# A hybrid retention, delta-rule and latent-attention trunk: SiLU kept until the next tile's copy, squares by chunk, three banks for projections, modulation jobs moved out of the attention

## The chip, the cores and the metric

The kernel runs on one core of a Trainium2 chip. The metric is the device time of one execution in microseconds, the median of several runs. TensorE does the matrix products, VectorE and ScalarE the elementwise work, GpSimd some additions; SyncE's queue issues most transfers. Below they are PE, DVE, ACT, POOL and SP in rows of the profile.

## What is computed

The reference is a trunk of two layers over 512 latent tokens and 256 context tokens of width 2048. In each layer a modulated norm is followed by one input projection, three groups of heads, a gate, one output projection and a residual with a modulated gate:

```python
shift, scale, gate = jnp.split(jax.nn.silu(c) @ ada_w[i] + ada_b[i], 3, axis=-1)
shift_c, scale_c, gate_c = jnp.split(jax.nn.silu(c_ctx) @ ada_w[i] + ada_b[i], 3, axis=-1)
h = rmsnorm(x, norm_w[i]) * (1.0 + scale[:, None]) + shift[:, None]
hc = rmsnorm(xc, norm_w[i]) * (1.0 + scale_c) + shift_c
zl = split_cols(h @ w_in[i], IN_SPLITS)
zc = split_cols(hc @ w_in[i], IN_SPLITS)
ret_c, ret_l = retention_mixer(...)
gdn_c, gdn_l = gated_deltanet_mixer(...)
mla_c, mla_l = mla_mixer(...)
x = x + gate[:, None] * (jnp.concatenate([ret_l, gdn_l, mla_l], axis=-1) @ w_out[i])
if not last:
    xc = xc + gate_c * (jnp.concatenate([ret_c, gdn_c, mla_c], axis=-1) @ w_out[i])
```

The delta group runs a centred convolution of five taps and a SiLU over its queries, keys and values, a chunked delta rule in both directions with their outputs added, a norm over the head and a SiLU gate. In the last layer the context is not projected for queries and gates, since only the latent tokens are an output.

## The kernel before, in words

Everything lies transposed: a tile has 128 channels on the partitions and the 768 tokens along the row, first the 256 of the context, then the 512 latent ones. A projection of 128 columns takes 16 tiles of the 2048 inputs. Each fp32 operand is split in a high and a low part (`split`, line 234 on ScalarE and 235 on VectorE), and three products are accumulated: a `zl` matmul of 512 columns (line 291) and, where the context is wanted, a `zc` matmul of 256 (line 293) for each.

Each layer has three stages: the mixing stage (`phase_a`), the latent attention (`phase_b`) and the output projection with the next layer's norm (`phase_c`). In the mixing stage every projection is a task, a generator that yields after each of its 16 steps (`proj_steps`): convolutions of the delta heads (`conv_task`), gates (`gate`), latent queries and keys (`latent`), retention inputs (`ret_raw`, `ret_v`). The heads' own code (`gdn_head`, then `ret_head`) calls `pump(us)` between its steps, which pulls about so many microseconds of projection steps from the tasks in their order, and `need(...)`, which runs the named tasks to their end. So TensorE has projection matmuls between the dependent steps of a head. The instructions then go through a scheduler that works by the program's order and its own model of durations; each engine carries out its list in order.

A head of the delta group ends in a chain of six steps (`chain`), in each of which two chunks of 128 tokens are finished, one per direction; the second to come to a chunk adds into `on` (line 1001, VectorE). `out_norm` then squares `on` by chunk (line 684, ScalarE), takes the root (396 to 401), scales (695, VectorE), and after `pump(6)` turns it (`ot`, line 692, TensorE).

A finished projection is copied out of its bank: the latent part by ScalarE (line 393, for convolutions 778), the context part by VectorE. A gate then runs its SiLU (413 to 421: four ScalarE and two VectorE instructions) and is stored; a convolution is first multiplied and added (780 on ScalarE, 782 four times on VectorE). Projections of the mixing stage take PSUM banks from a ring of four, `pza`; `m` tiles have four more banks.

The modulation of the next layer is computed on the side, in 64 jobs (`ada_job`): 16 multiplies on ScalarE (line 496), seven or eight additions on GpSimd (line 498) and four loads of 256 KB each. After each four jobs their sums are closed and turned by small matmuls. Jobs are called from projections in the mixing stage of layer 0 (36 calls), in its attention (16) and in its output projection (14). The first 16 jobs are the residual gate of layer 0, 32 the shift and scale of layer 1, the last 16 the residual gate of layer 1.

## Time and profile before

| quantity | value |
|---|---|
| runs of the kernel | median 3235.6 us of 3 (3230.44 to 3240.53) |
| the profiled execution | 3233.15 us, span 3231.4 us |
| TensorE's mean granted clock | 0.976 of full speed |
| TensorE busy | 3057.6 us, 95% of the span |
| VectorE, ScalarE, GpSimd busy | 2034.7 us (63%), 1639.7 us (51%), 701.9 us (22%) |
| stages: start, mixing 0, attention 0, output 0 | to 191, to 1320, to 1623, to 1906 us |
| stages: mixing 1, attention 1, output 1 | to 2713, to 3022, to the end |

The span runs from the first to the last instruction of the profiled execution. An engine is busy while an instruction of its own runs; matrix products are pipelined, so a busy TensorE may still run at a lower clock. A wait is an idle time of an engine, named after the instruction that came after it and what released that. In a table by stretch each line gives the stretch, its length, the busy time of PE, PEld (weight loads), DVE, ACT and POOL with the number of their instructions, then TensorE's granted clock as a share of full speed, the busy share of the DMA engines and their GB/s. In a table of groups a line gives line, engine, operation, output and inputs, shapes and count, then busy time and mean ns of one, then idle time of the engine just before them.

### The profile page before, as it was taken

How to read it: one execution, taken by the hardware profiler on the slowest of the kernel's cores; microseconds unless marked ns; L12 is line 12 of the kernel's file. 1: busy time of each engine (PE TensorE's matmuls, PEld its weight loads, DVE VectorE, ACT ScalarE, POOL GpSimd, SP SyncE). 2: the span in 40 equal slices, each digit the busy share in tenths (PEclk: the TensorE clock that was granted, in tenths of full speed). 3: DMA queues.
4: the chain of work that ended last, by engine and by line, in shares of the span. 5: the costliest groups of instructions: out<-in, count | busy, mean ns of one | idle time of the engine just before them, and what ended most of it. 6: DMA issues, size and time to landing. Idle time of an engine off the chain costs nothing.

```text
span 3231.4 us, 50867 instructions
## 1 busy us (share of the span) xinstructions
PE 3057.6 (95%) x18925; PEld 2582.6 (80%) x18925; DVE 2034.7 (63%) x3512; ACT 1639.7 (51%) x3492; POOL 701.9 (22%) x487
## 2 busy tenths in 40 slices
PE   7988979899899999999999999999999999999998
PEld 3477868788778778888878887888898887888887
DVE  3268567585675676676763265766766667766634
ACT  4266264453645666677776355352515245544533
POOL 0026043241344442255577300000000000000000
PEclk8999989999899999999999999999999999999999
DMA  8765243342344555333475443332424256512434
GB/s 286 254 207 144 52 145 92 87 133 71 121 123 134 162 179 179 109 107 106 140 228 160 121 120 95 91 98 69 119 58 124 66 157 177 155 52 64 134 113 132
DMA packets 506447, 417.06 MB, mean 129 GB/s; under 512 B 46454, under 2 KB 436694, under 8 KB 506198
## 3 DMA queue, kind: packets, MB, share of 16 engines
q1 hardware_dynamic: 505875, 413.70, 42.9%
q8 instruction: 148, 2.42, 0.3%
q14 instruction: 101, 0.83, 0.1%
q0 software_dynamic: 96, 0.02, 0.0%
q10 hardware_dynamic: 227, 0.08, 0.0%
HBM read 349.82 MB, written 63.88 MB: 128 GB/s over the span
## 4 chain that ended last, share of the span: by engine, by line
PE 48%; ACT 2%; DVE 1%; DMA 1%; issue 1%; POOL 1%; SPq 0%; ACTq 0%; DVEq 0%; POOLq 0%
PE zl L291 16%; PE zlc L291 9%; PE vz L274 4%; PE zc L293 3%; PE sc L1288 2%; PE zlc L293 2%; PE oacc L1347 2%; PE zt L282 2%; DMA gb<-g_d 1%; PE ptp L1340 1%; PE f L291 1%; POOL ada_a L498 1%; PE racc L1105 1%; PE chain L974 0%; PE f L293 0%
## 5 line engine op out<-in xcount | busy, mean ns | idle before, releaser
L498 POOL TENSOR_TENSOR ada_a<-ada_a,ada_p 128x512 f32<-128x512 f32 x480 | 699.9, 1458 | 1114.5 <-ACT ada_p L496 789.3
L235 DVE TENSOR_TENSOR wl<-raw,wh 128x512 fp32r<-128x512 f32 x632 | 477.6, 761 | 265.7 <-ACT wh L234 230.1
L291 PE MATMUL zl<-hh,wh 128*128 128x512 f32 (+1 forms) x1440 | 591.8, 411 | 8.8 <-ACT cz L778 7.0
L291 PE MATMUL zl<-hl,wh 128*128 128x512 f32 (+1 forms) x1440 | 578.0, 401 | 1.0 <-DVE hl L235 1.0
L291 PE MATMUL zl<-hh,wl 128*128 128x512 f32 (+1 forms) x1440 | 577.9, 401 | 0.0
L234 ACT CAST wh<-raw 128x512 fp32r<-128x512 f32 x632 | 373.2, 605 | 274.3 <-PE zc L293 134.2
L496 ACT ACTIVATE ada_p<-araw,const_f 128x256 f32<-128x256 f32 x960 | 423.8, 503 | 61.2 <-DMA araw<-in_ada_w_dram 46.5
L291 PEld LDWEIGHTS zl<-hh,wh 128*128 128x128 f32 (+1 forms) x1440 | 274.1, 190 | 66.7 <-ACT cz L778 7.4
L291 PEld LDWEIGHTS zl<-hl,wh 128*128 128x128 f32 (+1 forms) x1440 | 273.4, 190 | 60.5 <-DVE hl L235 2.5
L291 PEld LDWEIGHTS zl<-hh,wl 128*128 128x128 f32 (+1 forms) x1440 | 273.2, 190 | 60.5 <-issue 0.8
L293 PE MATMUL zc<-hh,wh 128*128 128x256 f32 (+1 forms) x960 | 280.1, 292 | 0.0
L293 PE MATMUL zc<-hh,wl 128*128 128x256 f32 (+1 forms) x960 | 277.3, 289 | 0.0
L293 PE MATMUL zc<-hl,wh 128*128 128x256 f32 (+1 forms) x960 | 277.2, 289 | 0.0
L293 PEld LDWEIGHTS zc<-hh,wh 128*128 128x128 f32 (+1 forms) x960 | 183.8, 191 | 3.9 <-issue 2.5
L293 PEld LDWEIGHTS zc<-hh,wl 128*128 128x128 f32 (+1 forms) x960 | 182.9, 191 | 3.0 <-issue 2.5
L293 PEld LDWEIGHTS zc<-hl,wh 128*128 128x128 f32 (+1 forms) x960 | 183.2, 191 | 1.7 <-issue 0.8
L291 PE MATMUL zlc<-ml,wh 128*128 128x512 f32 x448 | 178.0, 397 | 2.7 <-DVE ml L235 2.7
L291 PE MATMUL zlc<-mh,wl 128*128 128x512 f32 x448 | 178.0, 397 | 0.0
L291 PE MATMUL zlc<-mh,wh 128*128 128x512 f32 x448 | 177.8, 397 | 0.0
L782 DVE SCALAR_TENSOR_TENSOR cy<-cz,const_f,cy 128x770 f32<-128x770 f32 (+1 forms) x96 | 113.2, 1180 | 25.0 <-ACT cy L780 23.8
L291 PEld LDWEIGHTS zlc<-ml,wh 128*128 128x128 f32 x448 | 84.3, 188 | 24.5 <-DVE ml L235 5.4
L291 PEld LDWEIGHTS zlc<-mh,wh 128*128 128x128 f32 x448 | 84.5, 189 | 20.3 <-issue 0.8
(1249 smaller groups left out, 6456.5 us busy)
## 6 DMA issues: line engine op xcount, KB each, us to landing
raw<-in_w_in_dram SPq DMA_DIRECT2D x368, 256.0 KB, 3.7
araw<-in_ada_w_dram SPq DMA_DIRECT2D x256, 256.0 KB, 4.0
raw<-in_w_out_dram SPq DMA_DIRECT2D x144, 256.0 KB, 3.8
ar<-in_ada_w_dram SPq DMA_DIRECT2D x128, 256.0 KB, 5.2
x_d<-xt SPq DMA_DIRECT2D x32, 384.0 KB, 3.2
raw<-in_w_in_dram SPq DMA_DIRECT2D x72, 128.0 KB, 3.0
ret_d<-rw SPq DMA_DIRECT2D x20, 384.0 KB, 3.0
rz<-ret_d SPq DMA_DIRECT2D x20, 384.0 KB, 3.4
```

Of the source, the lines that this page charges most:

```text
L234: S.copy(hi, src)
L235: V.tensor_tensor(out=lo, in0=src, in1=hi.bitcast(F32), op=ALU.subtract)
L274: T.matmul(z[:, 256 * i:256 * i + 256], lhsT=x_[:, (j + i) * P:(j + i + 1) * P], rhs=w, start=first and k == 0 and i == 0, stop=end and k ...
L282: T.matmul(z, lhsT=w, rhs=xx[:, a:b], start=own and first and k == 0, stop=own and last and k == nk - 1)
L291: T.matmul(zl[:m], lhsT=w, rhs=xx[:, NX:], start=st, stop=sp)
L293: i = T.matmul(zc[:m, :NX], lhsT=w, rhs=xx[:, :NX], start=st and zc_open, stop=sp and zc_open)
L496: S.activation(out=pr[:, v], in_=raw[:, i, :], func=AF.Copy, scale=cs32[:, 2 * k + v:2 * k + v + 1])
L498: G.tensor_tensor(out=acc, in0=acc, in1=pr, op=ALU.add)
L782: V.scalar_tensor_tensor(out=y[:, lo:hi], in0=z[:, lo + o:hi + o], scalar=w(2 + o), in1=y[:, lo:hi], op0=ALU.mult, op1=ALU.add)
L1105: T.matmul(acc[:, :NL], lhsT=a[:, sl], rhs=b[:, :NL], start=st and i == 0, stop=sp and i == NCH - 1)
L1288: T.matmul(m[:, po:po + n], lhsT=a[:, qs], rhs=b[:, ko:ko + n], start=i == 0, stop=i == len(ops) - 1)
L1347: T.matmul(acc[:, os], lhsT=a[:, sl], rhs=b[:, js], start=j == 0 and n == 0, stop=j == nk - 1 and n == 2)
```

## The change

- The SiLU of a convolution or a gate, with its store, is kept in a list (`tails`) and issued behind the copy of the next tile that leaves its bank (`flush`), at the end of `need`, or at the end of the stage.
- The convolution's input has a buffer of its own with three parts of 260 columns, so the copy of the latent part becomes two of 258 columns; its result goes to one store instead of two; the zeros at the edges are written behind the previous tile's additions.
- The squares of `on` follow each addition into it. `out_norm` pumps 5 ahead of the scaling and 4 behind it, instead of 6 behind; in the retention heads a `pump(3)` becomes `pump(4)`.
- The mixing stage's projections take their banks from the ring `z` of three. The first groups of a layer use another split of banks.
- The attention calls no jobs. The 16 last jobs then fall into the mixing stage of layer 1.
- `load_params(1)` moves from the start to the head of the mixing stage of layer 0, and row paddings go.

```diff
     def pza(name="z"):
-        return ps.tile([P, 512], F32, name=name, tag="za", bufs=4)
+        return ps.tile([P, 512], F32, name=name, tag="z", bufs=3)
 
...
         hs = []
-        za, zb, zc2 = pm("f1"), ps.tile([P, 512], F32, name="f2", tag="f2", bufs=1), pz("zc2")
-        zs = [(pz("zl"), zc2[:, :NX]), (pz("zl"), zc2[:, NX:] if l < DEPTH - 1 else None),
-              (za[:, :512], zb[:, :NX]), (za[:, 512:], zb[:, NX:512])]
-        spare.append(ps.tile([P, 512], F32, name="spare", tag="spare", bufs=1))
+        f = lambda n: ps.tile([P, 512], F32, name=n, tag="f2", bufs=3)
+        z0, z1, zc2, za, zb, zc3 = pz("zl"), pz("zl"), pz("zc2"), f("f0"), f("f1"), f("f2")
+        zs = [(z0, zc2[:, :NX]), (z1, zc2[:, NX:] if l < DEPTH - 1 else None), (za, zc3[:, :NX]), (zb, zc3[:, NX:512])]
+        if l == 0:
+            spare.append(ps.tile([P, 512], F32, name="spare", tag="spare", bufs=1))
         owner = (1, 2) if l < DEPTH - 1 else (0, 2)
...
             V.tensor_scalar(out=dst[:m, 0:NX], in0=zc[:m, :NX], scalar1=scale, scalar2=None, op0=ALU.mult)
-        S.activation(out=dst[:m, NX:NT], in_=zl[:m], func=AF.Copy, scale=scale)
+        return S.activation(out=dst[:m, NX:NT], in_=zl[:m], func=AF.Copy, scale=scale).ins
 
...
         V.tensor_scalar(out=ngx, in0=ngx, scalar1=-1.0, scalar2=None, op0=ALU.mult)
-        load_params(1)
         return hs
...
 
+            tails, behind = [], [None]
+
+            def flush(ins=None):
+                fs, tails[:] = tails[:], []
+                for f in fs:
+                    if ins is None:
+                        f()
+                    else:
+                        with tc.issue_after(ins):
+                            f()
+
             def gate(c0, j):
                 lo_ctx = not last
                 zl, zc = yield from proj_in(l, c0, hs, lo_ctx)
                 z, e = ev("gz"), ev("ge")
                 lo = 0 if lo_ctx else NX
-                evac(z, zl, zc)
-                silu_mul(z[:, lo:], z[:, lo:], e[:, lo:])
-                dma(out=gate_d[l][j][:, lo:], in_=z[:, lo:])
+                flush(evac(z, zl, zc))
+
+                def tail():
+                    silu_mul(z[:, lo:], z[:, lo:], e[:, lo:])
+                    dma(out=gate_d[l][j][:, lo:], in_=z[:, lo:])
+                tails.append(tail)
 
...
                 lo = 0 if need_ctx else NX
-                evac(e, zl, zc)
+                flush(evac(e, zl, zc))
                 if kind not in accs:
...
 
-            def token_rstd(src, c0, sq, fill_v):
-                ss, y, t = tiny("nss"), tiny("nry"), tiny("nrt")
-                for n in range(c0, NCH):
-                    S.activation(out=sq[:, n * P:(n + 1) * P], in_=src[:, n * P:(n + 1) * P], func=AF.Square,
-                                 accum_out=ss[:, n:n + 1])
+            def square_chunk(src, n, sq, ss):
+                S.activation(out=sq[:, n * P:(n + 1) * P], in_=src[:, n * P:(n + 1) * P], func=AF.Square,
+                             accum_out=ss[:, n:n + 1])
+
+            def token_rstd(src, c0, sq, fill_v, ss=None):
+                y, t = tiny("nry"), tiny("nrt")
+                if ss is None:
+                    ss = tiny("nss")
+                    for n in range(c0, NCH):
+                        square_chunk(src, n, sq, ss)
                 fill_v(ss[:, c0:])
...
 
-            def out_norm(o, lo, wcol, j, fill_v=mean_eps, pump=lambda us: None):
+            def out_norm(o, lo, wcol, j, fill_v, pump, sq, ss=None):
                 c0 = lo // P
                 g = mk("og")
                 dma(out=g[:, lo:NT], in_=gate_d[l][j][:, lo:])
-                sq = mk("osq")
-                r = token_rstd(o, c0, sq, fill_v)
+                r = token_rstd(o, c0, sq, fill_v, ss)
+                pump(5)
                 scale_tokens(sq, o, r, c0)
-                pump(6)
+                pump(4)
                 m = pm("ot")
...
                 zl, zc = yield from proj_in(l, C_GDN + 512 * which + h * P, hs, need, False)
-                z, y, e = (w_(tag, name, n=NPAD) for tag, name in (("ev", "cz"), ("t", "cy"), ("t", "ce")))
-                lo, hi = (2 if need else LPAD), LPAD + NL
-                for o in (0, NX + 2, hi)[0 if need else 1:]:
-                    V.memset(z[:, o:o + 2], 0.0)
+                z, y = wk.tile([P, 1024], F32, name="cz", tag="cv", bufs=2), ev("cy")
+                z3, y3 = (t[:, :3 * n].rearrange("p (k c) -> p k c", k=3) for t, n in ((z, 260), (y, NX)))
+                s0 = 0 if need else 1
+                lo = s0 * NX
                 if need:
-                    V.tensor_copy(z[:, 2:2 + NX], zc[:, :NX])
-                S.copy(z[:, LPAD:hi], zl)
+                    behind[0] = V.tensor_copy(z3[:, 0, 2:258], zc[:, :NX]).ins
+                with tc.issue_after(behind[0]):
+                    for a, b in ((0, 2), (258, 262), (778, 780))[s0:]:
+                        V.memset(z[:, a:b], 0.0)
+                S.copy(z3[:, 1, 2:260], zl[:, :258])
+                flush(S.copy(z3[:, 2, :258], zl[:, 254:]).ins)
                 w = lambda j: parB[:, 12 * j + 4 * which + h:12 * j + 4 * which + h + 1]
-                S.activation(out=y[:, lo:hi], in_=z[:, lo:hi], func=AF.Copy, scale=w(2))
+                S.activation(out=y3[:, s0:], in_=z3[:, s0:, 2:258], func=AF.Copy, scale=w(2))
                 for o in (-2, 2, -1, 1):
-                    V.scalar_tensor_tensor(out=y[:, lo:hi], in0=z[:, lo + o:hi + o], scalar=w(2 + o),
-                                           in1=y[:, lo:hi], op0=ALU.mult, op1=ALU.add)
-                silu_mul(z[:, lo:hi], y[:, lo:hi], e[:, lo:hi])
-                if need:
-                    dma(out=conv_d[l][h][which][:, :NX], in_=z[:, 2:2 + NX])
-                dma(out=conv_d[l][h][which][:, NX:], in_=z[:, LPAD:hi])
+                    i = V.scalar_tensor_tensor(out=y3[:, s0:], in0=z3[:, s0:, 2 + o:258 + o], scalar=w(2 + o),
+                                               in1=y3[:, s0:], op0=ALU.mult, op1=ALU.add)
+                behind[0] = i.ins
+
+                def tail():
+                    silu_mul(y[:, lo:], y[:, lo:], z[:, lo:NT])
+                    dma(out=conv_d[l][h][which][:, lo:], in_=y[:, lo:])
+                tails.append(tail)
 
...
                 St, seen = [None] * 2, set()
+                osq, oss = mk("osq"), tiny("oss")
                 orders = ([0, 1, 2, 3, 4, 5], [1, 0, 5, 4, 3, 2])
...
                                 V.tensor_tensor(out=on[:, sl], in0=on[:, sl], in1=pp[d][:, 3 * P:], op=ALU.add)
+                                square_chunk(on, n, osq, oss)
                         if not end:
                             St[d] = S2[d]
                     pump(1)
                 ahead = gdn_load(h + 1) if h < 3 and need("conv", h + 1) else None
                 out_norm(on, qlo, parB[:, 71:72], 4 + h, lambda ss: V.scalar_tensor_tensor(
-                    out=ss, in0=ss, scalar=1.0 / HD, in1=qv[:, c0:], op0=ALU.mult, op1=ALU.add), pump)
+                    out=ss, in0=ss, scalar=1.0 / HD, in1=qv[:, c0:], op0=ALU.mult, op1=ALU.add), pump, osq, oss)
                 return ahead
...
                     split(ph[:, :w], pl[:, :w], p_[:, :w])
-                    pump(3)
+                    pump(4)
                     for a, b, st, sp in ((vh, ph, True, False), (vh, pl, False, False), (vl, ph, False, True)):
...
                 turn(m, o, qlo // P)
-                out_norm(m, qlo, parB[:, 70:71], h, pump=pump)
+                out_norm(m, qlo, parB[:, 70:71], h, mean_eps, pump, mk("osq"))
 
...
                 owed[0] = max(owed[0], -4.0)
+                flush()
                 return True
...
             mg = lambda a, b: [task(("mg", j), gate(C_MG + j * P, 8 + j)) for j in range(a, b)]
+            if not last:
+                load_params(1)
             gs = kr_ab()
...
                 advance(next(iter(tasks)))
+            flush()
 
...
                         first_half(h + 1, 0)
-                    if u and not last:
-                        ada_job()
                     for _ in range(PARTS[last][u]):
```

The order of the instructions moves at these places.

ScalarE at the end of delta head 0 in layer 0. `on` is the head's output, `nss` and `oss` hold the sums of squares, `ce` and `cz` are convolution tiles, `ada_p` a product of a job. Before:

```order
L413 ACTIVATE ce<-cy 128x770
L496 ACTIVATE ada_p<-araw,const_f 128x256
L414 ACTIVATE ce<-ce 128x770
L415 ACTIVATE ce<-ce,const_f 128x770
L234 CAST wh<-raw 128x512
L417 ACTIVATE ce<-ce 128x770
L684 ACTIVATE osq,nss<-on 128x128 x5
L234 CAST wh<-raw 128x512
L684 ACTIVATE osq,nss<-on 128x128
```

Now:

```order
L801 ACTIVATE cy<-cz,const_f 128x768
L694 ACTIVATE osq,oss<-on 128x128 x2
L1005 COPY vnew<-chain 128x128
L232 CAST wh<-raw 128x512
L1005 COPY vnew<-chain 128x128
L694 ACTIVATE osq,oss<-on 128x128 x2
L395 ACTIVATE nry<-oss 128x6
L396 ACTIVATE nry<-nry 128x6
```

The squares stood behind the SiLU of the third of three convolution tiles; they now stand two by two in the chain (`vnew` is one of its copies), and the root follows the last two.

ScalarE at a convolution tile of layer 0. Before, with copy, product and SiLU of the same tile:

```order
L778 COPY cz<-zl 128x512
L496 ACTIVATE ada_p<-araw,const_f 128x256
L780 ACTIVATE cy<-cz,const_f 128x770
L496 ACTIVATE ada_p<-araw,const_f 128x256 x5
L234 CAST wh<-raw 128x512
L496 ACTIVATE ada_p<-araw,const_f 128x256 x5
L413 ACTIVATE ce<-cy 128x770
L414 ACTIVATE ce<-ce 128x770
L234 CAST wh<-raw 128x512
L415 ACTIVATE ce<-ce,const_f 128x770
L417 ACTIVATE ce<-ce 128x770
```

Now, where lines 412 to 416 are the SiLU of the tile before, and its result of line 801 is left for the next:

```order
L798 COPY cz<-zl 128x258
L799 COPY cz<-zl 128x258
L412 ACTIVATE cz<-cy 128x768
L801 ACTIVATE cy<-cz,const_f 128x768
L413 ACTIVATE cz<-cz 128x768
L495 ACTIVATE ada_p<-araw,const_f 128x256
L414 ACTIVATE cz<-cz,const_f 128x768
L495 ACTIVATE ada_p<-araw,const_f 128x256 x2
L232 CAST wh<-raw 128x512
L416 ACTIVATE cz<-cz 128x768
L495 ACTIVATE ada_p<-araw,const_f 128x256 x6
```

The SiLU behind a copy now reads a `cy` whose four additions on VectorE belong to the tile before.

TensorE where a projection of the mixing stage of layer 0 follows another. Before, with a bank each for `zl_5739` and `zc_5740`:

```order
L291 MATMUL zl_5478<-hl15_1383,wh_5671 128x512
L293 MATMUL zc_5479<-hl15_1383,wh_5671 128x256
L291 MATMUL zl_5478<-hh15_1382,wl_5672 128x512
L974 MATMUL chain_5628<-r_5630,Xt32_5227 128x128
L293 MATMUL zc_5479<-hh15_1382,wl_5672 128x256
L291 MATMUL zl_5739<-hh0_641,wh_5743 128x512
L293 MATMUL zc_5740<-hh0_641,wh_5743 128x256
L291 MATMUL zl_5739<-hl0_642,wh_5743 128x512
```

Now:

```order
L289 MATMUL zl_6138<-hl15_1384,wh_6350 128x512
L291 MATMUL zc_6139<-hl15_1384,wh_6350 128x256
L289 MATMUL zl_6138<-hh15_1383,wl_6351 128x512
L291 MATMUL zc_6139<-hh15_1383,wl_6351 128x256
L289 MATMUL zl_6389<-hh0_642,wh_6393 128x512
L289 MATMUL zl_6389<-hl0_643,wh_6393 128x512
L289 MATMUL zl_6389<-hh0_642,wl_6394 128x512
L289 MATMUL zl_6389<-hh1_650,wh_6393 128x512
L291 MATMUL zc_6390<-hh0_642,wh_6393 128x256
L291 MATMUL zc_6390<-hl0_643,wh_6393 128x256
L291 MATMUL zc_6390<-hh0_642,wl_6394 128x256
```

The `zc` matmuls of a new tile stood between its `zl` matmuls from the first; four `zl` matmuls now come ahead of the first `zc`, whose bank is the one that the tile before leaves.

## Rows read from the trace of the kernel before

**Rows 1.** Table by stage: busy time of each engine, granted clock, DMA share; seven stages, five shown.

```profile
191.00:1320.00 1129.00, 1033.49 (x6742) 894.03 (x6742) 769.36 (x1157) 606.73 (x1338) 395.71 (x267) 0.96 0.42 126
1320.00:1623.00 303.00, 288.39 (x1873) 254.51 (x1872) 222.12 (x398) 228.25 (x513) 159.97 (x115) 0.98 0.38 119
1623.00:1906.00 283.00, 280.28 (x1598) 240.35 (x1598) 118.07 (x153) 152.42 (x320) 140.30 (x95) 0.99 0.52 159
1906.00:2713.00 807.00, 793.54 (x5132) 673.51 (x5131) 547.73 (x1094) 338.57 (x691) 0.00 (x0) 0.99 0.37 104
2713.00:3022.00 309.00, 307.36 (x1784) 264.85 (x1783) 218.89 (x411) 161.50 (x322) 0.00 (x0) 1.00 0.36 105
```

**Rows 2.** TensorE's waits, mixing stage of layer 0: total, times, longest, in us.

```profile
PE ot L692 <- DVE osq L695: 17.4, 4, 14.0
PE ot L692 <- ACT ge L413: 11.8, 1, 11.8
...
PE ktp L692 <- DVE kn L695: 9.8, 3, 6.2
PE vnp L812 <- ACT nry L397: 7.8, 1, 7.8
PE zl L291 <- ACT cz L778: 7.0, 1, 7.0
PE vtp L892 <- DVE vt L885: 6.2, 6, 2.1
PE vtp L905 <- DVE Xt L876: 6.0, 4, 2.0
```

**Rows 3.** TensorE's timeline, end of delta head 0: start, us, instruction, idle time before.

```profile
445.60 0.39 PE L291 MATMUL zl<-hh,wl 128*128 128x512 f32 x1
...
445.95 0.40 PE L291 MATMUL zl<-hh,wh 128*128 128x512 f32 x1
460.30 1.51 PE L692 MATMUL ot<-const_f,osq 128*128 128x128 f32 x6 [13.95 <-DVE osq L695]
```

**Rows 4.** VectorE's timeline, last `on` addition of head 0 and its scaling.

```profile
399.68 0.29 DVE L1001 TENSOR_TENSOR on<-on,chain 128x128 f32<-128x128 f32 x1 [0.86 <-PE chain L996]
...
459.19 0.96 DVE L695 TENSOR_TENSOR osq<-on,nss 128x768 f32<-128x768 f32 x1
```

**Rows 5.** ScalarE's timeline, first of head 0's six squares.

```profile
450.87 0.31 ACT L684 ACTIVATE osq<-on 128x128 f32<-128x128 f32 x1 [1.03 <-DVE cz L421]
```

**Rows 6.** Busy time and granted clock in the 13.5 us behind the gap.

```profile
462.20:475.70 13.50, 13.50 (x78) 11.50 (x77) 11.54 (x23) 11.84 (x35) 2.23 (x2) 0.88 0.43 135
```

**Rows 7.** ScalarE's timeline, copy of a convolution tile out of its bank.

```profile
634.30 0.57 ACT L778 COPY cz<-zl 128x512 f32<-128x512 f32 x1
```

**Rows 8.** TensorE's waits, mixing stage of layer 1.

```profile
PE ot L692 <- DVE osq L695: 7.9, 3, 4.5
```

**Rows 9.** Busy time in the first 444 us of either mixing stage.

```profile
191.00:635.00 444.00, 397.39 (x2610) 341.04 (x2609) 306.81 (x476) 225.95 (x487) 147.14 (x97) 0.94 0.39 112
1906.00:2350.00 444.00, 433.94 (x2733) 363.65 (x2732) 312.76 (x651) 205.03 (x415) 0.00 (x0) 0.99 0.35 97
```

**Rows 10.** The page's groups by cost: the jobs' additions and multiplies.

```profile
L498 POOL TENSOR_TENSOR ada_a<-ada_a,ada_p 128x512 f32<-128x512 f32 x480 | 699.9, 1458 | 1114.5 <-ACT ada_p L496 789.3
...
L496 ACT ACTIVATE ada_p<-araw,const_f 128x256 f32<-128x256 f32 x960 | 423.8, 503 | 61.2 <-DMA araw<-in_ada_w_dram 46.5
```

**Rows 11.** VectorE's groups, mixing stage of layer 0: busy us, mean ns, idle before.

```profile
L235 DVE TENSOR_TENSOR wl<-raw,wh 128x512 fp32r<-128x512 f32 x189 | 163.2, 865 | 90.1 <-ACT wh L234 75.7 <-issue 10.4 <-DMA araw<-in_ada_w_dram 1.6
```

**Rows 12.** VectorE's groups, mixing stage of layer 1.

```profile
L235 DVE TENSOR_TENSOR wl<-raw,wh 128x512 fp32r<-128x512 f32 (+1 forms) x185 | 125.7, 681 | 33.1 <-ACT wh L234 32.8
L782 DVE SCALAR_TENSOR_TENSOR cy<-cz,const_f,cy 128x770 f32<-128x770 f32 (+1 forms) x48 | 44.6, 929 | 12.6 <-ACT cy L780 12.0
```

**Rows 13.** VectorE's timeline, four additions of one convolution in layer 0.

```profile
437.02 6.94 DVE L782 SCALAR_TENSOR_TENSOR cy<-cz,const_f,cy 128x770 f32<-128x770 f32 x4 [2.39 <-ACT cy L780]
```

**Rows 14.** GpSimd's timeline beside them.

```profile
437.53 3.64 POOL L498 TENSOR_TENSOR ada_a<-ada_a,ada_p 128x512 f32<-128x512 f32 x2 [3.44 <-ACT ada_p L496]
```

More of the change, by code (lines that the diff above doesn't have):

```diff
@@ L47 @@
 COVER = (1.25, 1.0)
-LPAD = NX + 4
-NPAD = NT + 8
 def _rope_tables(dim):
@@ L138, in lslot @@
     def lslot(name, dt=F32R):
-        return lp.tile([P, NPAD], dt, name=name, tag="L")[:, :NT]
+        return lp.tile([P, NT], dt, name=name, tag="L")[:, :NT]
     BUFS = {"t": 5, "ev": 4, "p": 6, "d": 4, "xr": 1, "lacc": 1}
     def w_(tag, name, dt=F32, n=NT):
-        return wk.tile([P, NPAD * 4 // mybir.dt.size(dt)], dt, name=name, tag=tag, bufs=BUFS[tag])[:, :n]
+        return wk.tile([P, NT * 4 // mybir.dt.size(dt)], dt, name=name, tag=tag, bufs=BUFS[tag])[:, :n]
     mk = lambda name: w_("t", name)
@@ L215, in col_params @@
             o += r
-        p_ = pz("pst_ps")
+        p_ = zalloc[0]("pst_ps")
         T.transpose(p_[:, :P], st[:, :P], ident)
@@ L571, in start @@
                 src = ctxt[0, i * P:(i + 1) * P] if i < 2 else x[0, (i - 2) * P:(i - 1) * P]
-                n = lp.tile([P, NPAD], F32, name="xn", tag="L")[:, :512]
+                n = lp.tile([P, NT], F32, name="xn", tag="L")[:, :512]
                 dma(out=n, in_=src[:, qd * 512:(qd + 1) * 512])
                 xn.append(n)
-        bufs = [lp.tile([P, NPAD], F32, name=f"ar{i}", tag="L")[:, :512] for i in range(8)]
+        bufs = [lp.tile([P, NT], F32, name=f"ar{i}", tag="L")[:, :512] for i in range(8)]
         bufs += [hbuf(f"ar{8 + i}", 512, F32) for i in range(5)]
-        more = [lp.tile([P, NPAD], F32, name=f"ar{13 + i}", tag="L")[:, :512] for i in range(8)]
+        more = [lp.tile([P, NT], F32, name=f"ar{13 + i}", tag="L")[:, :512] for i in range(8)]
         wide = itertools.cycle(bufs + more)
@@ L1014, in ret_raw @@
                 z = ev("rw")
-                evac(z, zl, zc, scale=HD ** -0.5 if which == 1 else 1.0)
+                flush(evac(z, zl, zc, scale=HD ** -0.5 if which == 1 else 1.0))
                 dma(out=ret_d[l][h][which][:, lo:], in_=z[:, lo:])
```

## The prediction

> **What bounds the kernel now.** TensorE is the busiest engine, so I first read where it is not busy. The table by stage [rows 1] gives, for each stage, its length, TensorE's busy time and its granted clock. The reader is to see the difference of the first two: the mixing stage of layer 0 (191 to 1320 us) leaves 1129.0 - 1033.5 = 95.5 us idle, the attention of layer 0 leaves 303.0 - 288.4 = 14.6 us, the output projection 2.7 us, the mixing stage of layer 1 leaves 13.5 us, its attention 1.6 us. The attention of layer 0 differs from that of layer 1 in the clock too (0.98 against 1.00), and in GpSimd, busy 160.0 us in the one and not at all in the other.
>
> Second, TensorE's waits in the first mixing stage [rows 2]. The largest are those of the transposes `ot`: 17.4 us in four waits for `osq`, and 11.8 us in one that is put down to `ge`. Then come `kn`, `vT` (put down to `nry`), and one wait of 7.0 us of a projection for the copy that frees its bank. Third, one of these waits in time. Matmuls of a `zl`, `zc` pair follow each other every 0.35 us up to 445.95, and `ot` starts at 460.30 after 13.95 us of nothing [rows 3]. The last addition into `on` had begun at 399.68 and the scaling that `ot` waits for at 459.19 [rows 4]; the first square began at 450.87 [rows 5]. So the work was ready to be squared 51 us before ScalarE came to it: the squares stood in its order behind three convolution tiles.
>
> Fourth, the clock. In the 13.5 us behind that gap TensorE was busy all the time at a granted clock of 0.88, partly at the lower of the two levels, 1.2 GHz instead of 2.4 [rows 6]. Over the stage the clock of 0.96 is 0.04 x 1129 = 45 us, beside 95.5 us of idle time, so each us of long waiting costs 45 / 95.5 = 0.47 us more: factor 1.47. In layer 1 it is 0.01 x 807 = 8.1 us over 13.5: factor 1.6.
>
> **Squares in the chain (first mixing stage).** The squares now follow each `on` addition, and the square root stands directly behind the chain. Ahead of `ot` of head 0 TensorE then has 118 pairs of projection matmuls, 118 x 0.35 = 41 us, for heads 1 and 2 there are 65 and 50 pairs (23 and 18 us). From the first square to the end of the scaling it took 450.87 to 460.15, 9.3 us with other work between [rows 4, 5], which these cover. The waits of `ot` go: 17.4 + 11.8 = 29.2 us. The six squares of some 0.3 us now lie on ScalarE between the chain's copies; I cost them at nothing, since projection matmuls stand between the chain's steps too, and if that cover is gone each step is late by at most two squares, 0.6 us.
>
> **SiLU behind the next copy.** ScalarE no longer waits inside a tile's SiLU for that tile's own additions, so the copies that free banks come earlier. Of the waits in [rows 2] I take away the 7.0 us of `zl`, half of the 7.8 us of `vnp` (head 0's `vT` is stored earlier, but behind one more tile) and a third of the 9.8 us of `ktp`: 7.0 + 3.9 + 3.3 = 14.2 us. Bounds: none, and all 24.6. The extra copy of each convolution tile (24 tiles) is ScalarE work where that engine is 607 / 1129 = 54% busy: nothing.
>
> The sum of both is (29.2 + 14.2) x 1.47 = **-64 us**.
>
> **Three banks.** The context part of a tile now takes the bank that the latent part of the tile before it leaves, so it starts only when that bank's copy is done. The order has 17 hand-overs in this stage with under 1.5 us of TensorE work between the last matmul into a bank and the first into it again (5 before), and 23 with under 3 us (11 before). No row shows this wait by itself. The lower bound is a copy that starts at once, 0.57 us [rows 7] less the cover: near 0.4. The upper is the wait of 7.0 us [rows 2], with the copy queued behind other work. Nearest is the short end, since a convolution tile now makes two copies of about half a bank each, and the scheduler puts four or five `zl` matmuls ahead: I take 1.0 us for each of the 17, and 3 us at the head of the stage, where the decay chain and the first convolutions now share VectorE: **+20 us**, at no clock loss, as single short waits left the clock at 0.99 in the output projection [rows 1]. The Trainium skill ("TensorE: Matmul & The Clock Gate", A second HAM failure mode: psum-queue depth-cycling) says that a kernel which cycles through banks with many small idles loses clock by them. By that rule these 20 us would cost 0.47 x 20 = 9 us more, and the sum would be 3194 instead of 3185.
>
> **No jobs in the attention of layer 0.** Its 115 additions on GpSimd go [rows 1], and with them the multiplies on ScalarE that feed them. I take the attention of layer 1 as what remains: idle 14.6 to 1.6 us, -13.0, and clock 0.98 to 1.00, 0.02 x 303 = 6.1: **-19 us**. Bounds: 0, if the idle time belongs to the context's unit that only layer 0 has, and -19; I take the full size, because both engines that the jobs use are ones that attention waits for. The output projection keeps its jobs: 0. The two closings of modulation pairs that layer 1's norm needs now come near its end rather than in the attention; the last stands two output tiles ahead of the norm, which covers it.
>
> **The mixing stage of layer 1.** Its `ot` waits go as above: 7.9 us [rows 8] x 1.6 = -12.6 us. Sixteen jobs come in, some 17 ticks, all in the first 444 us of the stage. On ScalarE they are 256 x 0.503 = 129 us on top of 205, on GpSimd about 120 x 1.458 = 175 us where nothing was [rows 9, 10]. ScalarE then stands at 334 / 444 = 75%. VectorE has 312.8 us to do there. What GpSimd does to it: `wl` takes 865 ns in layer 0's stage [rows 11] and 681 in layer 1's [rows 12], 1.27 times. 312.8 x 1.27 = 397 us is 89% of 444. The stage has room on average but not at each place, so I give it the waits for VectorE that layer 0's stage has with such jobs: `ktp` 9.8, `vtp` 6.2 and 6.0 [rows 2], 22.0 us over four heads, three of which now have jobs beside them: 16.5 x 1.6 = **+26 us**. Bounds: 0 (TensorE's projections cover all of it) and +70 (rival D). Net +13.
>
> **Sum.** -64 + 20 - 19 + 26 - 13 = -50 us. The profiled execution took 3233.15 us (span 3231.4), 2.45 below the median of the runs, 3235.6. 3233.15 - 50 + 2.45 = 3185.6: forecast **3185 us**, and from 3167 to 3203 where the sizes of the terms move but their signs do not.
>
> **Rivals.**
> - **A, the new waits are hidden.** Copies are early enough for three banks, and VectorE has room in layer 1: without +17 and +26 it is 3185 - 17 - 26 = 3142 us. For it: 5 such hand-overs before, and one projection wait in [rows 2]. Against: it needs both at once. Chance 0.16.
> - **B, the waits move.** The transposes `knp` and `ktp` of the next head stand right behind `ot`, and their inputs come through the same two engines. If half to all of the 29.2 us shows up there, 14.6 to 29.2 x 1.47 comes back: 3206 to 3228 us. Against it: the scale of the next head's keys no longer queues behind late squares. Chance 0.15.
> - **C, the banks become the bound.** Each context tile's first matmuls wait for a copy that ScalarE or VectorE has not come to. At 3.5 us, half of the 7.0 seen, 23 x 3.5 x 1.47 = 118 us in place of 17: 3286 us. It decides the sign from ((50 + 17) / 1.47) / 23 = 2.0 us each. For it: three banks give the next tile no spare one. Against: the copy is 0.57 us, and stands ahead of the SiLU now. Chance 0.12.
> - **D, VectorE becomes the bound in layer 1.** Four additions of a convolution took 6.94 us with two GpSimd additions of together 3.64 us inside [rows 13, 14]; in layer 1 four take 4 x 0.929 = 3.72 on average [rows 12]. 3.72 + 3.64 = 7.36, so the two engines went almost by turns. If all of VectorE's work met GpSimd so, 312.8 + 175 = 488 us stands against 444: +44 for the stage, and with factor 1.6 +70, in place of +26: 3203 to 3229 us, and higher if work that VectorE puts off delays the retention heads too. The Trainium skill ("SBUF — State Buffer", Who interferes with whom) gives the cause: an instruction of VectorE with two inputs in SBUF and one of GpSimd that reads SBUF use one shared port, and the second to issue blocks until the first is done; the row agrees. Against the full price: layer 0's stage has jobs at nearly the same rate in its first part (147.1 us of GpSimd in 444 [rows 9]), and `wl` was 1.27 times as long there, not twice. Chance 0.12.
>
> **How the numbers follow.** Forecast 0.45, A 0.16, B 0.15, C 0.12, D 0.12. 0.3% is 9.7 us, about what a measurement tells from no change. Below 3225.9 lie the forecast, A, 0.13 of B, 0.01 of C and 0.05 of D: faster 0.80. Within 3225.9 to 3245.3: 0.02 of B, 0.02 of C, 0.05 of D: 0.09. Above: 0.09 of C, 0.02 of D: 0.11. The range from 3128 to 3245 us leaves out those 0.11 and the far end of A, some 0.04.
>
> **What would show it.** Right: no `ot` wait above 2 us in the list of waits; the first mixing stage near 1085 us with a clock of 0.98; the attention of layer 0 near 284 us with GpSimd idle; the mixing stage of layer 1 near 820 us, with waits of `ktp` and `vtp` for VectorE. Wrong: `zc` or `zl` waiting for `cz` or `ce` copies at more than 2 us each (C); VectorE over 95% in the first part of layer 1's stage with `zl` waiting for `wl` (D); `ktp` or `knp` with ten us or more in layer 0 (B).

## The result: slower by 0.6%, and the profile after

The changed kernel takes 3256.32 us, the median of five runs (3254.25 to 3261.0), against 3235.6 before. The ratio is 1.0063, with an interval of 1.0046 to 1.0079. The forecast was 3185, with a range up to 3245 us. The profiled execution took 3254.25 us, span 3252.4. The table by stage of the kernel after, with the columns of [rows 1], from the first mixing stage to the attention of layer 1:

```profile
188.00:1299.00 1111.00, 1030.31 (x6746) 891.77 (x6747) 753.84 (x1153) 602.06 (x1347) 403.17 (x268) 0.97 0.43 128
1299.00:1583.00 284.00, 276.97 (x1826) 249.26 (x1825) 203.05 (x410) 154.50 (x310) 19.39 (x15) 0.99 0.28 86
1583.00:1860.00 277.00, 276.98 (x1618) 239.99 (x1617) 107.63 (x159) 143.85 (x302) 121.19 (x90) 1.00 0.52 154
1860.00:2735.00 875.00, 822.77 (x5213) 691.89 (x5212) 607.60 (x1097) 432.76 (x940) 162.72 (x105) 0.97 0.40 114
2735.00:3046.00 311.00, 299.16 (x1726) 257.94 (x1725) 215.64 (x406) 155.35 (x313) 0.00 (x0) 0.98 0.34 100
```

The attention of layer 0 is 284 us long, as forecast. The first mixing stage is 1111 us, against 1129, where 1085 was forecast; 80.7 us are still idle. And the mixing stage of layer 1 is 875 us, against 807, where 820 was forecast: here lies the loss. VectorE is busy 60 us longer there than in [rows 1], with the same number of instructions within three, and GpSimd 163 us. TensorE's waits in that stage (engine, tile, what it waited for, total in us, times, longest) are many and small:

```profile
PE vtp L915 <- DVE vt L908: 9.9, 6, 3.0
PE ktp L709 <- DVE kn L712: 7.4, 3, 3.9
PE ot L709 <- DVE osq L712: 6.4, 1, 6.4
PE vtp L907 <- DVE Xt L894: 5.3, 3, 2.5
PE gcp L766 <- DVE const_f L760: 4.8, 1, 4.8
```

Most of them name VectorE. In the first mixing stage the waits of `ot` are gone but for 4.4 us, and others stand in their place; compare `ktp` with its 9.8 us in [rows 2]:

```profile
PE ktp L709 <- DVE kn L712: 14.4, 3, 6.7
PE racc L1130 <- ACT ph L232: 6.9, 2, 6.4
...
PE ktp L709 <- ACT et L867: 6.3, 1, 6.3
PE zl L289 <- DVE cz L794: 5.6, 1, 5.6
PE knp L709 <- issue: 5.4, 1, 5.4
...
PE ot L709 <- ACT ada_e L523: 4.4, 1, 4.4
```

### The profile page after: what moved, and what is told of

It reads as the page before. It is cut to its first block, busy times and chain, and to the rows that moved or that the text cites. A ratio compares the mean times of both kernels' runs of the same rounds, so it can differ in the third digit from the quotient of the medians.

```text
span 3252.4 us, 50824 instructions
## 1 busy us (share of the span) xinstructions
PE 3056.7 (94%) x18925; PEld 2583.9 (79%) x18925; DVE 2044.4 (63%) x3512; ACT 1638.3 (50%) x3516; POOL 711.0 (22%) x487
## 5 line engine op out<-in xcount | busy, mean ns | idle before, releaser
L497 POOL TENSOR_TENSOR ada_a<-ada_a,ada_p 128x512 f32<-128x512 f32 x480 | 709.1, 1478 | 1625.0 <-ACT ada_p L495 1307.1
L233 DVE TENSOR_TENSOR wl<-raw,wh 128x512 fp32r<-128x512 f32 x632 | 492.6, 785 | 245.6 <-ACT wh L232 212.0
L803 DVE SCALAR_TENSOR_TENSOR cy<-cz,const_f,cy 128x768 f32<-128x768 f32 (+1 forms) x96 | 109.2, 1137 | 14.5 <-ACT cy L801 14.0
```

Source lines behind the costliest of these rows:

```text
L233: V.tensor_tensor(out=lo, in0=src, in1=hi.bitcast(F32), op=ALU.subtract)
L497: G.tensor_tensor(out=acc, in0=acc, in1=pr, op=ALU.add)
L803: i = V.scalar_tensor_tensor(out=y3[:, s0:], in0=z3[:, s0:, 2 + o:258 + o], scalar=w(2 + o), in1=y3[:, s0:], op0=ALU.mult, op1=ALU.add)
```

## The experiments

Stages are compared from here on between marks that every kernel has: a mixing stage runs from its first transposition `abp` to the first score `sc` of the attention, the attention to the first `zlc` matmul, the output projection to the next `abp`. Each cell gives the stage's length, then TensorE's idle time in it, both in us, from the profiled execution; the ratio is of the runs to those of the kernel before taken beside them (medians of 3228 to 3232 us; 3236 for the changed kernel), with its interval.

| kernel | time, ratio | mixing 0 | attention 0 | output 0 | mixing 1 |
|---|---|---|---|---|---|
| before | 3235.6 | 1156, 96 | 276, 14 | 351, 4 | 840, 13 |
| changed | 3256.3, 1.0063 (1.0046 to 1.0079) | 1138, 83 | 257, 5 | 342, 1 | 912, 62 |
| jobs back in the attention | 3227.7, 0.9985 (0.9971 to 0.9998) | 1144, 87 | 283, 17 | 351, 5 | 847, 20 |
| no additions in layer 1 | 3198.1, 0.9900 (0.9876 to 0.9924) | 1137, 81 | 257, 5 | 342, 1 | 854, 22 |
| no multiplies in layer 1 | 3259.6, 1.0090 (1.0065 to 1.0116) | 1140, 81 | 254, 3 | 342, 1 | 917, 62 |
| jobs in output projection | 3248.0, 1.0051 (1.0035 to 1.0067) | 1137, 83 | 267, 8 | 394, 38 | 848, 21 |
| before, squares alone | 3223.5, 0.9975 (0.9958 to 0.9991) | 1149, 88 | 277, 14 | 352, 6 | 834, 10 |
| before, three banks alone | 3237.1, 1.0015 (1.0000 to 1.0031) | 1166, 103 | 274, 12 | 351, 4 | 839, 13 |
| jobs back, four banks | 3228.3, 0.9996 (0.9982 to 1.0010) | 1141, 86 | 278, 12 | 352, 4 | 844, 19 |
| the same, more cover for ktp | 3215.1, 0.9948 (0.9933 to 0.9962) | 1136, 81 | 277, 14 | 352, 5 | 846, 20 |
| changed, no additions at all | 3099.1, 0.9609 (0.9581 to 0.9636) | 1037, 14 | 256, 5 | 343, 1 | 854, 22 |
| before, no additions at all | 3090.3, 0.9579 (0.9548 to 0.9610) | 1039, 16 | 258, 3 | 345, 1 | 842, 15 |
| before, squares, no additions | 3094.8, 0.9574 (0.9548 to 0.9600) | 1041, 14 | 257, 3 | 345, 1 | 836, 11 |
| changed, sums on TensorE | 3181.7, 0.9866 (0.9836 to 0.9896) | 1089, 15 | 256, 3 | 361, 1 | 874, 22 |
| the same, more cover for ktp | 3200.5, 0.9916 (0.9886 to 0.9946) | 1106, 24 | 256, 3 | 361, 1 | 878, 25 |
| before, sums on TensorE | 3175.2, 0.9819 (0.9788 to 0.9850) | 1091, 19 | 281, 2 | 355, 1 | 844, 15 |
| before, squares, sums on TensorE | 3163.9, 0.9791 (0.9766 to 0.9815) | 1082, 14 | 281, 2 | 355, 1 | 841, 11 |

### Are the moved jobs the loss in layer 1?

The first kernel puts the job calls back:

```diff
+                    if u and not last:
+                        ada_job()
                     for _ in range(PARTS[last][u]):
```

> The changed kernel with one part undone: the attention of layer 0 calls its sixteen jobs again, so none is left for the mixing stage of layer 1. In the trace of the changed kernel that stage takes 875 us against 807 before, and the attention of layer 0 takes 284 against 303. If the sixteen jobs are what slows layer 1 (rival D of the prediction): its mixing stage falls to 790 to 810 us, the attention goes back to about 300, and the time is near 3256 - 68 + 19 = 3207 us. If the three banks and the kept SiLU slow layer 1 (rival C): its mixing stage stays near 860 us and the time is near 3265.

The mixing stage of layer 1 falls from 912 to 847 us, the attention goes back to 283. So the sixteen jobs cost 65 us in the one place and 26 in the other, with 9 more in the output projection. The rows of the stage in the changed kernel and in the one with the jobs back:

```profile
1925.20:2836.90 911.70, 850.05 (x5281) 713.51 (x5281) 637.12 (x1131) 435.39 (x943) 151.43 (x97) 0.97 0.42 119
```

```profile
1964.90:2812.10 847.20, 827.18 (x5232) 701.57 (x5232) 576.05 (x1127) 354.41 (x737) 0.00 (x0) 0.98 0.39 112
```

The time is 21 us above the expected 3207: the price of the old place was not 19 but 35, and the first mixing stage, where nothing was edited, took 6 us more.

What in a job costs that? Two kernels leave out half of it each: the first the additions, the second all multiplies but the first of each sum, so that GpSimd adds the loaded rows themselves.

```diff
-                if k:
+                if k and not (l == 1 and s >= 16):
                     G.tensor_tensor(out=acc, in0=acc, in1=pr, op=ALU.add)
```

> The changed kernel, in which the sixteen jobs in the mixing stage of layer 1 leave out their additions on GpSimd (the residual gate of layer 1 is then not the reference's) and keep their loads and their 256 multiplies on ScalarE. From the start of that stage to the first score of the attention the changed kernel takes 912 us, without any jobs there 847. If GpSimd blocking VectorE is the cost (rival D): 850 to 865 us, time 3256 - 52 = 3204 us. If it is the multiplies in ScalarE's order ahead of copies and weight casts: 890 to 912 us, time 3235 to 3256.

```diff
+                if k and l == 1 and s >= 16:
+                    G.tensor_tensor(out=acc, in0=acc, in1=raw, op=ALU.add)
+                    continue
                 pr = acc if k == 0 else wk.tile([P, 2, 256], F32, name="ada_p", tag="ada_p", bufs=2)
```

> The counterpart: the sixteen jobs keep their additions on GpSimd, which now add the loaded rows themselves, and leave out all multiplies but the 16 first ones of the accumulators (the residual gate of layer 1 is again not the reference's). If GpSimd blocking VectorE is the cost: the stretch stays at 895 to 912 us, time 3240 to 3256. If ScalarE's multiplies are: 850 to 870 us, time 3200 to 3215. If both share it, both kernels lie near 880.

Without additions the stage takes 854 us, without multiplies 917. The two rows of the table by stretch, first without additions, then without multiplies:

```profile
1924.90:2778.70 853.80, 831.79 (x5281) 703.51 (x5281) 577.63 (x1131) 432.85 (x944) 0.00 (x0) 0.98 0.45 127
```

```profile
1925.20:2842.40 917.20, 855.12 (x5280) 719.15 (x5280) 652.44 (x1131) 363.27 (x753) 147.60 (x96) 0.95 0.41 119
```

ScalarE's 433 us of work in the first kernel, against 363, cost next to nothing; GpSimd's 148 us in the second cost all of it. This speaks against another cause too, that GpSimd holds up ScalarE by taking the products late: in the second kernel there are no products to take, and the stage is as long; in the changed kernel ScalarE waits for GpSimd 7.5 us in the whole stage. VectorE has 1131 instructions in both, and is busy 578 and 652 us. Its groups in the changed kernel and in the one without additions (busy us, mean ns, idle before) answer to [rows 12]:

```profile
L233 DVE TENSOR_TENSOR wl<-raw,wh 128x512 fp32r<-128x512 f32 (+1 forms) x194 | 152.2, 788 | 44.7 <-ACT wh L232 37.4 <-DMA araw<-in_ada_w_dram 7.1
L803 DVE SCALAR_TENSOR_TENSOR cy<-cz,const_f,cy 128x768 f32<-128x768 f32 (+1 forms) x48 | 49.3, 1027 | 7.2 <-ACT cy L801 7.0
L899 DVE TENSOR_TENSOR X<-vt,const_f 128x768 f16<-128x768 f16 x40 | 26.5, 696 | 0.7
```

```profile
L233 DVE TENSOR_TENSOR wl<-raw,wh 128x512 fp32r<-128x512 f32 (+1 forms) x194 | 131.2, 680 | 49.8 <-ACT wh L232 47.9 <-DMA vT<-conv_d 1.6
L803 DVE SCALAR_TENSOR_TENSOR cy<-cz,const_f,cy 128x768 f32<-128x768 f32 (+1 forms) x48 | 44.4, 924 | 7.7 <-ACT cy L801 7.4
L899 DVE TENSOR_TENSOR X<-vt,const_f 128x768 f16<-128x768 f16 x40 | 20.8, 554 | 0.6
```

The same instructions go back to the lengths of a stage without GpSimd, 680, 924 and 554 ns. How one addition holds VectorE shows best where the instruction itself is nearly nothing. VectorE's timeline in the changed kernel, at the root of head 1's keys in layer 0, and GpSimd's beside it:

```profile
458.27 0.16 DVE L829 TENSOR_SCALAR nss<-nss 128x6 f32<-128x6 f32 x1
...
461.62 1.22 DVE L398 TENSOR_TENSOR nrt<-nrt,nss 128x6 f32<-128x6 f32 x1
...
463.03 1.23 DVE L399 TENSOR_SCALAR nrt<-nrt 128x6 f32<-128x6 f32 x1
...
464.77 1.22 DVE L400 TENSOR_TENSOR nss<-nry,nrt 128x6 f32<-128x6 f32 x1
...
466.18 0.94 DVE L712 TENSOR_TENSOR kn<-knp,nss 128x768 f32<-128x768 f32 x1
```

```profile
461.44 4.53 POOL L497 TENSOR_TENSOR ada_a<-ada_a,ada_p 128x512 f32<-128x512 f32 x3 [0.16 <-ACT ada_p L495]
```

An instruction on 128 x 6 numbers takes 0.16 us at 458.27. Beside three additions of 4.53 us the next three of that size take 1.22, 1.23 and 1.22 us: each ends as an addition ends, and these three lie one behind the other ahead of `kn`, for which `ktp` waits. Not every instruction is held: `A<-kkp,const_f,es`, which reads one of its tensors from PSUM, takes 339 ns on average in the first mixing stage of the kernel before, where 28 of its 48 run beside an addition, and 342 ns in the same kernel without additions; `X<-vt,const_f`, with both in SBUF, takes 913 and 554 ns. The rule of the Trainium skill in rival D ("SBUF — State Buffer", Who interferes with whom), that the second to issue blocks until the first is done, agrees with these rows; `nrt<-nrt` has only one tensor in SBUF as its input and waited as long; the same section of the Trainium skill names its operation, tensor_scalar, among those that can take the shared ports.

### Where did the gain of the squares go?

The kernel before with the squares alone (the diff of the change in `token_rstd`, `out_norm`, the chain and the calls):

> The kernel before with the squares by chunk and the new pumps of the output norm alone. If the prediction's step holds by itself (29.2 us of ot waits gone, factor 1.47): 3235.6 - 43 - 12 = 3181 us. If the waits only move to the transposes of the next head's keys (rival B), half or less of it: 3205 to 3235 us, with ktp or knp waits of 15 us and more in the mixing stage of layer 0.

The waits of `ot` fall to 1.6 us, and the stage from 1156 to 1149. The waits of TensorE in it:

```profile
PE ktp L697 <- DVE kn L700: 22.2, 3, 8.0
PE racc L1112 <- ACT ph L234: 17.9, 4, 6.0
PE vnp L817 <- DMA vT<-conv_d: 7.6, 1, 7.6
...
PE knp L697 <- issue: 3.0, 1, 3.0
```

In the kernel before, `racc` (the retention heads' sums) had this line, and `knp` none:

```profile
PE racc L1105 <- ACT ph L234: 11.4, 4, 4.1
```

`ktp` went from 9.8 to 22.2 and `knp` from nothing to 3.0: 15.4 us, just over the half of 29.2 that rival B names. `racc` went from 11.4 to 17.9. More projection matmuls ahead of `ktp` should then help:

```diff
                 scale_tokens(kn, m, r, 0)
-                pump(4)
+                pump(9)
```

> The same with pump(9) in place of pump(4) between the scaling of the keys and the transposes ktp, which gives some 3 to 6 us more of projection matmuls ahead of ktp in each head. With three banks and pump(4), ktp waits 22.1 us in four in layer 0 since ot no longer waits. If a fixed latency from knp to ktp is where the gain of the squares went: ktp waits fall to 8 us or less, the mixing stage of layer 0 is 10 to 20 us shorter than with pump(4). If the time moves on again, to the retention heads that then lack projections (racc): within 5 us of it.

By the runs the time is 13 us less than with `pump(4)` (3215 against 3228); in the profiled executions it is 4 us, 5 of them in that stage, where 86 and 81 us are idle: `ktp` fell from 21.9 to 16.3 us, not to 8, and waits of `vtp` and for banks took it over. Whatever wait was taken away, 81 to 88 us of the 96 us of idle time stayed.

That floor is GpSimd's. Both kernels without any additions:

```diff
-                if k:
-                    G.tensor_tensor(out=acc, in0=acc, in1=pr, op=ALU.add)
```

> The changed kernel with all additions of the modulation jobs on GpSimd left out, in every stage (the modulation of layer 1 and the residual gate of layer 0 are then not the reference's); loads and multiplies stay. In layer 1 leaving them out gave back 58 us for 16 jobs. The mixing stage of layer 0 has 36 jobs and 1138 us, of which 83 are idle and 37 lost to the clock, whatever wait was taken away so far. If GpSimd blocking VectorE is behind that too: 1050 to 1080 us, time 3110 to 3145. If the idle time there is the heads' own latency: 1125 to 1138 us, time 3185 to 3198, as with the additions of layer 1 alone left out.

> The kernel before with the same additions left out. Beside the run above it shows what the rest of the change (squares, SiLU, banks, places of the jobs' multiplies) is worth without GpSimd. If that rest is worth the 25 to 45 us that the prediction gave it when nothing blocks VectorE: this kernel is 25 to 45 us above the run above. If the squares are worth nothing because the keys' latency comes right behind: within 10 us of it. The wait of ot for the squares, which stand behind three convolution tiles, should stay above 8 us in head 0 of layer 0 in either case.

The first mixing stages of the changed kernel without additions, of the kernel before without them, and of the kernel before itself:

```profile
191.40:1228.70 1037.30, 1023.84 (x6912) 893.03 (x6912) 631.87 (x1190) 618.22 (x1377) 0.00 (x0) 1.00 0.47 140
```

```profile
190.40:1229.40 1039.00, 1022.47 (x6912) 894.15 (x6911) 635.53 (x1185) 624.45 (x1384) 0.00 (x0) 0.99 0.47 141
```

```profile
190.90:1346.60 1155.70, 1059.33 (x6913) 917.49 (x6911) 787.69 (x1185) 630.62 (x1385) 404.48 (x274) 0.96 0.43 127
```

The first two are some 1038 us long, with a clock of 1.00 and 0.99 and 14 to 16 us idle. The scheduler sets the rest nearly as it was: in the kernel before, 2 to 3% of the instructions of TensorE and VectorE in this stage stand at another place without the additions. GpSimd's additions thus cost the kernel before 1156 - 1039 = 117 us in this stage for 274 of them, 0.43 us each, and the changed kernel 912 - 854 = 58 us in layer 1 for 97, 0.60 each (three of the sixteen jobs run ahead of that stage). In the first mixing stage of the kernel before VectorE is busy 788 us with the additions and 636 without. The waits of `ot`, which should have kept 8 us in head 0, are small too:

```profile
PE ot L690 <- DVE osq L693: 8.8, 2, 5.0
PE zl L291 <- ACT cz L776: 5.9, 1, 5.9
```

With nothing blocking VectorE the changed kernel is 9 us slower than the one before, by its mixing stage of layer 1, where the moved multiplies are: the rest of the change is worth nothing. Is that the squares?

> The kernel before with the squares by chunk alone, and all additions of the jobs on GpSimd left out (the modulation is then not the reference's). The kernel before without the additions took 3090 us, with 8.8 us of ot waits left in the mixing stage of layer 0 and 8.0 in layer 1. If the step was right but for GpSimd: ot waits gone and no new ktp or racc waits, 15 to 25 us less, 3065 to 3075 us. If the keys' latency takes the place of the waits in any case: 3085 to 3095.

They are worth nothing in time (ratios of 0.9574 and 0.9579 to the kernel before), as `ktp` takes over from `ot` here also:

```profile
PE ktp L695 <- DVE kn L698: 9.6, 3, 3.6
PE vnp L815 <- ACT lacc L545: 1.8, 1, 1.8
```

### The banks

The kernel before with `pza` on the ring of three and the new first groups:

> The kernel before with the three banks (and the other banks of the first groups) alone, SiLU and squares where they were. By the prediction's term: 17 hand-overs of 1.0 us, 3250 us. If the banks are the main cost (rival C), with each convolution's copy queued behind the SiLU of the tile before as it was: 3270 to 3300 us. If the scheduler hides them: within 5 us of 3236.

It is 0.15% slower, at the edge of its interval, with a wait of 10.3 us and others of `zc` for a late copy:

```profile
PE zc L293 <- DVE gz L393: 10.3, 1, 10.3
```

The other way round, four banks from the twelfth of a stage on, in the changed kernel with its jobs back:

```diff
     def pza(name="z"):
-        return ps.tile([P, 512], F32, name=name, tag="z", bufs=3)
+        pzn[0] += 1
+        if pzn[0] % 1000 < 12:
+            return pz(name)
+        return ps.tile([P, 512], F32, name=name, tag="za", bufs=4)
```

> The kernel with the jobs back in the attention, and in each mixing stage a ring of four banks from the twelfth bank on. With three banks its mixing stage of layer 0 takes 1144 us, with waits of zl and zc of 17.8 us in seven. If the third bank costs what these waits show, times 1.5: 1120 us, time near 3203. If the idle time moves to ktp and racc as that of ot did: 1135 to 1144, time 3218 to 3228.

3 us in the stage, nothing in the time. With the SiLU behind the copies three banks are enough; the waits that they cause are few (three of 3.4 to 5.6 us in the changed kernel) instead of 17 of 1 us.

### Another place, or another engine, for the sums

> The changed kernel with the sixteen jobs in another place: one job for each head in the attention of layer 0 (8) and two instead of one at each tick of the output projection of layer 0, where TensorE is busy 277 of 277 us and ScalarE and VectorE 52% and 39%. If a stage with room takes jobs for nothing: attention 8 to 10 us longer than without jobs, output projection 277 to 280 us, layer 1's mixing stage 790 to 810, time 3256 - 68 + 10 = 3198 us. If GpSimd becomes the bound there (24 jobs x 7.5 additions x 1.35 us = 243 of 277 us) and the norm of layer 1 waits: output projection 290 to 310 us, time 3215 to 3230.

Its edit calls `ada_job()` for the second of three units in the attention of layer 0 and twice at each tick of the output projection. The second theory came out, and worse: the stage grew by 51 us, with one line of waits behind it:

```profile
PE ada_q L530 <- ACT ada_e L524: 35.5, 5, 10.7
```

The small matmuls `ada_q` that close a pair stand in TensorE's order and need ScalarE's copy `ada_e` of the sums. In the longest of these waits the sums had left TensorE at 1638.1 us, and the copy began at 1651.1: it stands in ScalarE's order behind the next job's multiplies, and these waited for GpSimd 3.87 and 1.34 us.

Then the sums were given to TensorE itself, so that neither GpSimd nor ScalarE's multiplies are needed:

```diff
+                T.matmul(z[32 * g:32 * g + 32], lhsT=cs32[:, 2 * k:2 * k + 32], rhs=raw[:, i, :],
+                         start=j < 2, stop=j >= 2, tile_position=(0, 32 * g))
```

> The changed kernel with the jobs' sums made by TensorE: each job is eight matmuls of 256 columns into four groups of 32 rows of a bank of its own, in place of 16 multiplies on ScalarE and 7 or 8 additions on GpSimd. At the start of the kernel before eight such matmuls of 512 columns took 1.48 us in one place and two took 1.05 in others, so a job costs TensorE 0.7 to 2.1 us, all 64 jobs 47 to 134. Without GpSimd the mixing stage of layer 1 falls from 912 to 854 and takes 12 to 34 for its jobs: 866 to 888. If layer 0 gains as the run without additions is to show: 3256 - 58 - 70 + 47 to 134 = 3175 to 3260 us; if ScalarE's relief counts too, below that.

> The same with pump(9) in place of pump(4) ahead of the transposes ktp, which gave 13 us where GpSimd was at work. If the latency from knp to ktp was long because GpSimd blocked VectorE, the extra cover is worth less now: within 5 us of the same without it. If it is the chain's own length: 8 to 15 us less.

> The kernel before with the jobs' sums made by TensorE and nothing else. From the kernel before without additions, 3090 us, and 87 us of matmuls: 3177 us. If TensorE waits for the jobs' loads with a bank of the ring held: 3185 to 3210.

> The kernel before with the squares by chunk and the jobs' sums made by TensorE in banks of the stage's ring. The changed kernel with such sums took 3182 us; its TensorE had 87 us more work than without. If the squares alone are the useful part: 3070 + 87 = 3155, up to 3170 us. If the kept SiLU and the free eighth bank are needed: 3180 or more.

The changed kernel gains 2% on itself by this (3182 against 3256). Against the changed kernel without additions, TensorE's work, less idle time and clock losses, grows by 49 us in the first mixing stage, 19 in the output projection and 17 in layer 1, 85 us for 64 jobs or 1.3 us each. By the prices above a job's 7.5 additions cost 7.5 x 0.43 = 3.2 to 7.5 x 0.60 = 4.5 us. More cover for `ktp` was of no use here: the stage is 18 us longer with it, which neither expectation held. The kernel before gains as much, and with the squares it is the fastest of all that leave nothing out, 3163.9 us, 2.1% below the kernel before. Its first mixing stage:

```profile
184.60:1266.70 1082.10, 1068.56 (x7527) 918.91 (x7527) 636.93 (x1195) 411.79 (x825) 0.00 (x0) 1.00 0.45 133
```

1082 us with 13.5 idle, though TensorE does more. The squares are worth 11 us here (3164 against 3175), and both times are near what was expected.

## Why the prediction was wrong, step by step

- **No jobs in the attention of layer 0: right in the number, partly by luck.** Forecast -19, measured 276 - 257 = -19. But putting the jobs back alone costs 26 there (283): the term was worth -26, and the rest of the change added 7. The output projection gave 9 more, not forecast; TensorE is idle 1 us there instead of 4, and seven of its `oacc` matmuls now lie ahead of the mark; the rest of the 9 us is open.
- **The mixing stage of layer 1: the step that turned the sign.** Forecast +26 for the jobs, measured 912 - 847 = +65, of which 912 - 854 = 58 are the additions. The load was not underrated: 397 us was forecast for 313 of VectorE's work, and its busy time over the stage grew by 59.5 us, less than that. What failed is the passage from load to path. I charged only the waits that named VectorE in layer 0 (`ktp`, `vtp`), and put the largest other waits in the 95.5 us of idle time there down to the place of the squares and the SiLU. Without additions all but 16 us (by the marks, of 96) are gone. They were the price of 274 additions, and were spread over waits that name other things.
- **Rival D came, by its mechanism and not by its condition.** It gave +44 to +70, which holds the 65, but put it down to VectorE running out of time. VectorE is busy 637 of 912 us, 70%. 59.5 us more of VectorE gave 58 us of stage. The rows at `kn` show how that can be, three blocked instructions in one chain ahead of a transpose; that most of the 58 us came in this way is argued, not traced wait by wait.
- **Squares in the chain: forecast -43 in layer 0, measured -7 alone.** The waits of `ot` went, 29.2 to 1.6 us, as forecast; that 1.47 times as much would leave the stage did not follow. The keys' root, a chain of the same kind, comes next in TensorE's order (rival B), without GpSimd as well. The factor itself holds: the kernel before without additions loses 80 us of idle time and 117 of length, 1.46. The 13.95 us before `ot` was also no property of the order alone: without additions all `ot` waits of the stage are 8.8 us, with the squares still behind the three convolution tiles. In layer 1 the forecast was -13: squares alone took 840 to 834 us, but the whole change without the jobs took 847, and with them `ot` waits 13 us again. What makes the rest of the change 13 us dearer there is open.
- **SiLU behind the next copy and three banks: -21 and +20 forecast together as good as nothing, and so measured.** Squares, SiLU and banks together took the stage from 1156 to 1144 us, squares alone to 1149.
- **Sum.** Forecast -44, -19, 0, +13; measured -18, -19, -9, +72 by these marks, with -5 outside them: +21.

Not tried is the kernel before with nothing but the jobs moved from the attention to layer 1.

## What to carry to other kernels

Work on a side engine is not free because that engine and its neighbours have time left: price it by leaving it out once, in the stage where it runs, and not by the waits that carry its neighbour's name. When taking away the largest wait of a serial chain, ask how much of the next step's latency it was covering; if the idle time of a stage stays the same whatever wait is removed, look for what lengthens all of them. Sixteen multiplies and some additions on two other engines can be dearer than eight small matmuls on the engine that bounds the kernel.

## What was not expected of the hardware

- A VectorE instruction of 128 x 6 numbers took 1.22 us beside an addition of GpSimd and 0.16 without. In the first mixing stage of the kernel before 404 us of GpSimd lengthened VectorE's busy time from 636 to 788 us, 0.38 us per us, and the stage by 117.
- GpSimd's additions, when fed by loads alone, cost as much as those fed by ScalarE (917 and 912 us for the stage), and 433 - 354 = 79 us of multiplies on ScalarE alone cost 854 - 847 = 7.
- Eight matmuls of 256 columns into four groups of 32 rows cost 1.3 us in place of a job. The profile has two rows for each, 1024 for the 64 jobs, most of them 0.379 us long, 6.1 us for a job's sixteen; but they overlap, and where the sixteen follow each other, at 421.37 us, they span 1.07 us. (The expectation's eight and two matmuls at the start of the kernel before were such rows too, of four and of one.)

```profile
L502 PE MATMUL ada_z<-araw,const_f x1024: 379/379/634, 184.0 to 2257.2; 128*32 128x256 f32 x171
```
